# Pinning the order of TensorE's products in the attention of a two-mixer encoder layer

## The chip, the cores and the metric

One core of one Trainium2 chip runs one launch of the kernel. The metric is device microseconds of that launch: 922.22 us before the change, the median of 3 runs (920.89 to 922.51). Lower is better.

## The reference

One layer of a streaming encoder is applied to 512 prompt frames and 32 sample frames, 544 columns in all, with a model width of 1024. All data is float32.

```
h = rmsnorm(x)
z = h @ w_in            -> q_a k_a v_a q_b k_b v_b gate_a gate_b
q, k: RMS norm per head (head_dim 64)
mixer A: 16 q heads, 4 kv heads, own chunk of 64 and 2 before, ALiBi, a sink logit in the softmax
mixer B: 16 heads, own chunk and 8 before, learned bias by relative distance
x = x + (sigmoid(gate_a) * o_a + sigmoid(gate_b) * o_b) @ w_out
u = rmsnorm(x) @ w_up;  c = causal depthwise conv of width 3 over u;  [a | b] = c
x = x + (gelu(a) * b) @ w_down
```

It returns x and the new rows of the caches: k, v of both mixers and the last rows of u.

## The kernel before

Activations lie transposed, features on the 128 partitions and the 544 frames as columns. A projection (`dense`) makes 128 output features for all frames, in two halves of 272 columns. Every float32 operand is split into a rounded high part and a low rest, so each of the 8 blocks of a half takes three products (`triple`): high by high, high by low, low by high. A half is thus 24 products into one PSUM bank. The weights of a projection come by one DMA (`w_raw`), GpSimd rounds them (`w_hi`, L202; ScalarE does from the FFN on, L204), and VectorE makes the rest (`w_lo`, L205). Two buffers of each are there, so that a projection's weights are made while another's are used.

The first three projections run on rows that aren't normalised yet (`dense_first`), and are scaled when the norm is known. Somewhat later the rows are normalised in place (L255) and split again into the operands that the projections read (`row_split`, ScalarE L327, VectorE L328).

Attention is woven into the projections by hand. `Stream` has a clock of its own, which each queued product advances by its columns / 2350 us (at least 0.108; a transposition 0.109). A step of attention is a generator. It queues its products, then yields the time in which its next operands will be there (`LAT_...`), and is taken up again when the clock has come that far: `pe.step()` is called after each triple. The steps are these.

- `head_norm`: after each half of a q or k projection, ScalarE squares it (`t_sq`, L414), GpSimd splits the squares (`t_sqh`, `t_sql`, L416 and L417), and after `LAT_SQ` a product with `bdiag` sums them. ScalarE and VectorE make the root from it, GpSimd (L424) and VectorE (L425) scale, and q or k is written in two parts (L448, L449; L433, L434). `LAT_NORM` later it counts as ready, k after a further `LAT_DMA` for its copy to the other 64 partitions.
- `load_v`: `LAT_Z` after its projection v is transposed (L90).
- `attend_prompt`: a head's scores are made in four tiles, and VectorE adds the bias and finds the maxima (L504). The softmax (`nm` L485, exponentials L488, sums L492, reciprocal L494, scaling of p by GpSimd L496) is issued at a lower priority. `LAT_SOFT` later p is transposed (L90) and split (`pt_h`, `pt_l`, L514 and L515), and `LAT_PT` later come the products with v, an h part and an l part for each block, queued in one piece.
- `attend_sample` does the same for the 32 sample frames, with `LAT_SOFT_S` and `LAT_PTS`.

A head starts when its q, k and v are ready and `PACE_A` or `PACE_B` has passed since the one before. `reserve` holds a projection back while the buffers that it will need are taken. After the projections of mixer B (two for each group of gates at the end, `GATES_B`), `w_out` is begun while the last heads finish, and `pe.flush()` runs what is left.

The order so queued is not the order of the instructions on an engine. [...] 

The change touches the latencies (L55 to L59), `Stream`'s methods `matmul` and `transpose`, and the buffer counts in `head_norm`, `transposed` and `attend_prompt`.

Of the kernel before, what the change touches and what calls it, by code (L numbers as in the profile page):

```python
# [8 lines left out]
F32 = mybir.dt.float32  # L9
F32R = mybir.dt.float32r  # L10
# [42 lines left out]


LAT_FIRST, LAT_ROW = 9.15, 0.35  # L55
LAT_SQ, LAT_NORM, LAT_DMA = 2.9, 6.89, 3.63
LAT_Z, LAT_SOFT, LAT_PT = 6.55, 9.34, 4.75
LAT_SOFT_S, LAT_PTS = 8.46, 1.1
PACE_A, PACE_B, PACE_S = 7.09, 5.87, 1.44  # L59

WARM = 7
# [8 lines left out]
class Stream:  # L70
# [1 line left out]

    def __init__(self, nc):
        self.nc = nc
        self.clock, self.seq, self.next = 0.0, 0, 0.0
        self.tasks, self.heads = [], []
        self.live = {}

    def matmul(self, out, lhsT, rhs, **kw):
        n = 1
        for d in rhs.shape[1:]:
            n *= d
        self.clock += max(n / 2350, 0.108)
        return self.nc.tensor.matmul(out, lhsT=lhsT, rhs=rhs, **kw)  # L86

    def transpose(self, out, src, ident):
        self.clock += 0.109
        return self.nc.tensor.transpose(out, src, ident)  # L90

    def run(self, gen):
        for wait in gen:
# [50 lines left out]

def body(ctx, tc, a, o):
    nc = tc.nc
    pe = Stream(nc)
    mm, transpose = pe.matmul, pe.transpose
    act = nc.scalar.activation
    V, G = nc.vector, nc.gpsimd  # L150
# [11 lines left out]
    def bank(pool):  # L162
        return pool.tile([128, 512], F32, name="ps")
# [50 lines left out]
    def weights():  # L214
        n = state["used"]
        state["used"] += 1
        while state["prepped"] < min(n + 3, len(sources)):
            prep_next()
        return W.pop(n)

    def triple(ps, w, k, c0, cn, first, last):

        ks = slice(128 * k, 128 * k + 128)
        xs, xl = (x[:, c0:c0 + cn] for x in moving[k])
        mm(ps[:, :cn], lhsT=w[0][:, ks], rhs=xs, start=first, stop=False)
        mm(ps[:, :cn], lhsT=w[0][:, ks], rhs=xl, start=False, stop=False)
        mm(ps[:, :cn], lhsT=w[1][:, ks], rhs=xs, start=False, stop=last)
# [37 lines left out]
    def interleaved(halves, ks):  # L265

        for k in ks:
            for ps, w, s in halves:
                triple(ps, w, k, *HALVES[s], k == 0, k == KC - 1)
                pe.step()  # L270

    def dense_first(evac):


        early.append((evac, weights()))
        if len(early) < (FIRST if xt else 2):
            return
        halves = [(bank(psd if i < 3 else psa), early[i // 2][1], i % 2) for i in range(2 * len(early))]
        interleaved(halves[:3], range(KC))
        for h in halves[3:]:  # L280
            interleaved([h], range(KC))
        while not norm_done:
            pe.idle()
        for i, (ps, _, s) in enumerate(halves):
            c0, cn = HALVES[s]
            early[i // 2][0](s, c0, cn, ps[:, :cn])

    def leave(z, ps, c0, cn):

        if not scaled:  # L290
            state["left"] = V.tensor_tensor(z, ps, rstd[:, c0:c0 + cn], ALU.mult)
            return state["left"]
        return nc.scalar.copy(z, ps)
# [6 lines left out]
    ident = const.tile([128, 128], F32, name="ident")  # L300
# [12 lines left out]
    def newton(st, cn, pool):  # L313

        y = pool.tile([128, 272], F32, name="t_y")[:, :cn]
        act(y, st, AF.Ln, bias=eps)
        act(y, y, AF.Exp, scale=-0.5)  # L317
        b = pool.tile([128, 272], F32, name="t_b")[:, :cn]
        act(b, y, AF.Square)
        V.scalar_tensor_tensor(b, st, eps, b, ALU.add, ALU.mult)  # L320
        return b, y
# [9 lines left out]
    class RowNorm:  # L331


        def __init__(self, slots, tmp):
            self.slots, self.tmp, self.n, self.sums = slots, tmp, 0, []
            self.r = xp.tile([128, T], F32, name="rstd")
# [32 lines left out]
    ap = att.enter_context(tc.tile_pool(name="ap", bufs=2))  # L369
# [8 lines left out]
    xt = [slot() for _ in range(KC)]  # L378
# [24 lines left out]

    def head_norm(gi, write):
        def task(s, c0, cn, ps):
            z = ap.tile([128, 272], F32, name="z", bufs=4)[:, :cn]
            sq = ap.tile([128, 272], F32, name="t_sq", bufs=2)[:, :cn]
            sqh = ap.tile([128, 272], F32R, name="t_sqh")[:, :cn]
            sql = ap.tile([128, 272], F32R, name="t_sql")[:, :cn]
            gain = gains[:, gi:gi + 1]  # L410
            if not scaled:
                leave(z, ps, c0, cn)
                ps = z
            act(sq, ps, AF.Square)  # L414
            act(z, ps, AF.Identity, scale=gain)  # L415
            G.tensor_scalar(sqh, sq, 1.0, 1.0, ALU.mult, ALU.mult)  # L416
            G.tensor_tensor(sql, sq, rr(sqh), ALU.subtract)  # L417
            yield LAT_SQ
            st = bank(psa)[:, :cn]
            mm(st, lhsT=bdiag, rhs=sqh, start=True, stop=False)  # L420
            mm(st, lhsT=bdiag, rhs=sql, start=False, stop=True)
            b, y = newton(st, cn, ap)
            zn = ap.tile([128, 272], F32, name="zn")[:, :cn]
            G.tensor_tensor(z, z, y, ALU.mult)  # L424
            V.scalar_tensor_tensor(zn, b, -3.0, z, ALU.add, ALU.mult)  # L425
            write(s, c0, cn, zn)

        def evac(s, c0, cn, ps):
            pe.run(task(s, c0, cn, ps))
        return evac  # L430
# [67 lines left out]
    def scores(out, lhs, rhs, bias, floor, mx):  # L498
        ps = bank(psa)
        n = len(lhs)  # L500
        for i in range(n):
            mm(ps[:, :rhs[i].shape[1]], lhsT=lhs[i], rhs=rhs[i], start=i == 0, stop=i == n - 1)
        ps = ps[:, :out.shape[1]]
        V.tensor_tensor_reduce(out=out, in0=ps, in1=bias, op0=ALU.add, op1=ALU.max, scale=1.0,  # L504
                               scalar=floor, accum_out=mx)

    def transposed(p, blocks, n):

        ps = bank(psa)
        for src, dst in blocks:  # L510
            transpose(ps[:, dst:dst + 128], p[:, src:src + 128], ident)
        h = ap.tile([128, 512], F32R, name="pt_h", bufs=3)
        l = ap.tile([128, 512], F32R, name="pt_l", bufs=3)
        nc.scalar.copy(h[:, :n], ps[:, :n])  # L514
        V.tensor_tensor(l[:, :n], ps[:, :n], rr(h)[:, :n], ALU.subtract)  # L515
        return h, l

    def fold(po, dst, hh, n):

        own, other = ((slice(0, 64), slice(64, 128)), (slice(64, 128), slice(0, 64)))[hh]  # L520
        t = ap.tile([128, 512], F32, name="t_o", bufs=2)
        nc.scalar.copy(t[own, :n], po[other])
        V.tensor_tensor(dst[own], po[own], t[own, :n], ALU.add)
# [7 lines left out]
    def attend_prompt(q, kh, kl, bias, floor, sinkcol, geo, groups, vt, hh, dst, dh, scored, done):  # L531


        p = ap.tile([128, 1280], F32, name="p")
        mx = ap.tile([128, 4], F32, name="mx", bufs=4)
        tiles = []
        for t, (pc, k0, n, bc) in enumerate(geo):
            qs = q[:, 128 * t:128 * t + 128]
            scores(p[:, pc:pc + n], [qs, qs], [x[:, k0:k0 + max(n, 256)] for x in (kh, kl)], bias[:, bc:bc + n],
                   floor, mx[:, t:t + 1])  # L540
            tiles.append(slice(pc, pc + n))
        scored()
        with tc.high_priority(LATER):
            softmax(p, tiles, mx, sinkcol)
        yield LAT_SOFT
        pts = []
        for blocks, n, _ in groups:
            pts.append(transposed(p, blocks, n))
        yield LAT_PT
        po = bank(psa)  # L550
        started = False
        last = groups[-1][2][-1]
        for (h, l), (_, _, prods) in zip(pts, groups):
            for pr in prods:
                j, c, oc, w = pr
                for x in (h, l):
                    mm(po[:, oc:oc + w], lhsT=vt[:, j, hh, :, :], rhs=x[:, c:c + w],
                       start=not started, stop=pr is last and x is l, skip_group_check=True)
                    started = True
        fold(po, dst[:, :NP], dh, NP)  # L560
        done()
# [315 lines left out]
    for k in range(KC):  # L877
# [4 lines left out]
        if k >= lag:  # L882
            interleaved(halves[2:3], (k - lag,))
    pe.flush()
    interleaved(halves[2:3], range(KC - lag, KC))
    interleaved(halves[3:], range(KC))
    att.close()
# [18 lines left out]
    for i, (ps, _, s) in enumerate(halves):  # L906
        c0, cn = HALVES[s]
# [328 lines left out]
```

## Time and profile before

| | |
|---|---|
| median of 3 runs | 922.22 us (920.89 to 922.51) |
| the execution profiled | 921.02 us |
| its span, first to last instruction | 919.2 us |
| granted TensorE clock, mean | 0.996 |
| TensorE products busy | 895.1 us (97%), 7085 instructions |
| TensorE weight loads busy | 881.3 us (96%) |
| VectorE busy | 720.0 us (78%) |
| ScalarE busy | 540.5 us (59%) |
| GpSimd busy | 378.2 us (41%) |

PE stands for TensorE's products, PEld for its weight loads, DVE for VectorE, ACT for ScalarE, POOL for GpSimd. Products are pipelined and their ends are modelled, so they overlap in the records. Idle time of an engine counts in the waits only where it is over 0.15 us. Attention and its projections run to some 475 us; `w_out`'s remainder and the FFN follow.

### The profile page before, as it was taken

How to read it: one execution, taken by the hardware profiler on the slowest of the kernel's cores; microseconds unless marked ns; L12 is line 12 of the kernel's file. 1: busy time of each engine (PE TensorE's matmuls, PEld its weight loads, DVE VectorE, ACT ScalarE, POOL GpSimd, SP SyncE). 2: the span in 40 equal slices, each digit the busy share in tenths (PEclk: the TensorE clock that was granted, in tenths of full speed). 3: DMA queues.
4: the chain of work that ended last, by engine and by line, in shares of the span. 5: the costliest groups of instructions: out<-in, count | busy, mean ns of one | idle time of the engine just before them, and what ended most of it. 6: DMA issues, size and time to landing. Idle time of an engine off the chain costs nothing.

```text
span 919.2 us, 18903 instructions
## 1 busy us (share of the span) xinstructions
PE 895.1 (97%) x7085; PEld 881.3 (96%) x7085; DVE 720.0 (78%) x1470; ACT 540.5 (59%) x1283; POOL 378.2 (41%) x577
## 2 busy tenths in 40 slices
PE   7979999999999999999999999999999999999998
PEld 6979999989989999999999999999999999999998
DVE  7798867777988888997856568677787776886996
ACT  5668887778878677777663244334444433534542
POOL 4625548466867767765541213222222221100100
PEclk9999999999999999999999999999999999999999
DMA  7222133312344343343415222222222222232342
GB/s 223 90 89 87 53 96 92 112 58 82 109 133 125 113 145 106 124 126 120 134 47 189 83 79 92 93 92 80 82 93 92 92 90 76 93 107 78 117 146 67
DMA packets 40012, 94.38 MB, mean 103 GB/s; under 512 B 4944, under 2 KB 16240, under 8 KB 39920
## 3 DMA queue, kind: packets, MB, share of 16 engines
q1 hardware_dynamic: 39920, 93.17, 31.9%
q8 instruction: 56, 0.92, 0.4%
q14 instruction: 36, 0.29, 0.1%
HBM read 80.48 MB, written 7.10 MB: 95 GB/s over the span
## 4 chain that ended last, share of the span: by engine, by line
PE 78%; DVE 8%; ACT 3%; POOL 3%; issue 2%; DMA 0%; DVEq 0%; POOLq 0%; ACTq 0%
PE ps L86 75%; PE ps L90 3%; DVE q L449 1%; ACT p L488 1%; DVE w_lo L205 1%; DVE p L504 1%; POOL p L496 1%; DVE zn L425 1%; DVE s L255 1%; DVE t_b L320 1%; POOL t_sql L417 1%; DVE k L434 0%; POOL z L424 0%; DVE xl L328 0%; DMA k<-k 0%
## 5 line engine op out<-in xcount | busy, mean ns | idle before, releaser
L86 PE MATMUL ps<-xh,w_lo 128*128 128x272 f32 x1536 | 445.3, 291 | 5.6 <-DVE w_lo L205 5.6
L86 PE MATMUL ps<-xh,w_hi 128*128 128x272 f32 x1536 | 444.5, 291 | 2.8 <-ACT z L415 1.7
L86 PE MATMUL ps<-xl,w_hi 128*128 128x272 f32 x1536 | 444.5, 290 | 0.4 <-DVE xl L328 0.3
L86 PEld LDWEIGHTS ps<-xh,w_lo 128*128 128x128 f32 x1536 | 290.3, 189 | 7.0 <-DVE w_lo L205 6.5
L86 PEld LDWEIGHTS ps<-xh,w_hi 128*128 128x128 f32 x1536 | 290.1, 189 | 4.6 <-ACT z L415 1.9
L86 PEld LDWEIGHTS ps<-xl,w_hi 128*128 128x128 f32 x1536 | 290.6, 189 | 1.5 <-DVE xl L328 1.1
L205 DVE TENSOR_TENSOR w_lo<-w_raw,w_hi 128x1024 fp32r<-128x1024 f32 (+2 forms) x112 | 143.0, 1277 | 32.6 <-ACT w_hi L204 18.7
L202 POOL TENSOR_SCALAR w_hi<-w_raw 128x1024 fp32r<-128x1024 f32 (+2 forms) x62 | 67.0, 1082 | 92.9 <-PE ps L86 69.2
L496 POOL TENSOR_SCALAR p<-p,rc 128x256 f32<-128x256 f32 (+3 forms) x128 | 74.7, 601 | 41.3 <-DVE rc L494 37.9
L204 ACT CAST w_hi<-w_raw 128x1024 fp32r<-128x1024 f32 x50 | 52.6, 1051 | 64.8 <-issue 36.0
L86 PE MATMUL ps<-s,w_hi 128*128 128x272 f32 x448 | 84.0, 288 | 0.0
L488 ACT ACTIVATE p<-p,nm 128x256 f32<-128x256 f32 (+3 forms) x128 | 65.4, 513 | 28.0 <-DVE nm L485 27.9
L942 POOL TENSOR_SCALAR state_u<-u 128x2 f32<-128x2 f32 x44 | 17.1, 389 | 145.5 <-DVE u L939 145.5
L86 PE MATMUL ps<-s 128*128 128x272 f32 (+1 forms) x483 | 71.3, 293 | 1.7 <-DVE s L374 1.7
L86 PEld LDWEIGHTS ps<-s,w_hi 128*128 128x128 f32 x448 | 70.0, 188 | 0.0
L939 DVE TENSOR_TENSOR u<-ps,rstd 128x272 f32<-128x272 f32 x88 | 38.5, 440 | 39.6 <-PE ps L86 36.9
L86 PEld LDWEIGHTS ps<-s 128*128 128x128 f32 x483 | 65.0, 190 | 2.2 <-DVE s L374 1.7
L86 PE MATMUL ps<-s,w_lo 128*128 128x272 f32 x224 | 63.7, 288 | 0.0
L86 PE MATMUL ps<-k,q 128*128 128x256 f32 (+2 forms) x256 | 52.2, 308 | 3.3 <-DMA k<-k 1.6
L417 POOL TENSOR_TENSOR t_sql<-t_sq,t_sqh 128x272 fp32r<-128x272 f32 x52 | 52.6, 1012 | 3.7
L424 POOL TENSOR_TENSOR z<-z,t_y 128x272 f32<-128x272 f32 x52 | 42.7, 822 | 21.9 <-ACT t_y L317 19.9
L515 DVE TENSOR_TENSOR pt_l<-ps,pt_h 128x512 fp32r<-128x512 f32 (+1 forms) x80 | 45.6, 602 | 5.5 <-ACT pt_h L514 4.3
(164 smaller groups left out, 1627.3 us busy)
## 6 DMA issues: line engine op xcount, KB each, us to landing
w_raw<-in_w_in SPq DMA_DIRECT2D x50, 512.0 KB, 3.4
w_raw<-in_w_up SPq DMA_DIRECT2D x44, 512.0 KB, 3.3
w_raw<-in_w_pair SPq DMA_DIRECT2D x16, 512.0 KB, 3.3
k<-k SPq DMA_DIRECT2D x40, 128.0 KB, 2.3
bias<-in_rel SPq DMA_DIRECT2D x16, 256.0 KB, 2.9
w_raw<-in_w_out SPq DMA_DIRECT2D x8, 512.0 KB, 3.4
s<-in_x SPq DMA_DIRECT2D x15, 272.0 KB, 5.7
w_raw<-in_w_down SPq DMA_DIRECT2D x6, 512.0 KB, 3.3
```

Of the source, the lines that this page charges most:

```text
L86: return self.nc.tensor.matmul(out, lhsT=lhsT, rhs=rhs, **kw)
L90: return self.nc.tensor.transpose(out, src, ident)
L202: G.tensor_scalar(hi[:, c], raw[:, c], 1.0, 1.0, ALU.mult, ALU.mult)
L204: nc.scalar.copy(hi[:, c], raw[:, c])
L205: V.tensor_tensor(lo[:, c], raw[:, c], rr(hi)[:, c], ALU.subtract)
L417: G.tensor_tensor(sql, sq, rr(sqh), ALU.subtract)
L424: G.tensor_tensor(z, z, y, ALU.mult)
L488: act(p[:, sl], p[:, sl], AF.Exp, bias=nm[:, t:t + 1], accum_out=sm[:, t:t + 1])
L496: G.tensor_scalar(p[:, sl], p[:, sl], rc[:, t:t + 1], 1.0, ALU.mult, ALU.mult)
L515: V.tensor_tensor(l[:, :n], ps[:, :n], rr(h)[:, :n], ALU.subtract)
L939: V.tensor_tensor(u[:, 2 + c0:2 + c0 + cn], ps, rstd2[:, c0:c0 + cn], ALU.mult)
L942: G.tensor_scalar(state_u[:, m, 0:2], u[:, NP:NP + 2], 1.0, 1.0, ALU.mult, ALU.mult)
```

## The change

`Stream` takes the tile context and gets a flag, `strict`. While it is set, each product and each transposition that goes through `Stream` is passed to `keep_in_program_order`, which adds an edge of order, without a wait, to the engine's instruction traced before it. So TensorE's list is the order in which they were queued. The flag is set at the end of the first three projections, before their results are evacuated, and cleared after `pe.flush()`. The same function runs a second time for the FFN, where `xt` is empty and the flag stays off.

Seven of the latencies are raised, and seven tiles get more buffers.

```diff
-LAT_SQ, LAT_NORM, LAT_DMA = 2.9, 6.89, 3.63
-LAT_Z, LAT_SOFT, LAT_PT = 6.55, 9.34, 4.75
-LAT_SOFT_S, LAT_PTS = 8.46, 1.1
+LAT_SQ, LAT_NORM, LAT_DMA = 4.2, 8.0, 3.63
+LAT_Z, LAT_SOFT, LAT_PT = 7.0, 10.8, 5.4
+LAT_SOFT_S, LAT_PTS = 9.5, 2.3
...
-        return self.nc.tensor.matmul(out, lhsT=lhsT, rhs=rhs, **kw)
+        return self.keep(self.nc.tensor.matmul(out, lhsT=lhsT, rhs=rhs, **kw))
...
-        return self.nc.tensor.transpose(out, src, ident)
+        return self.keep(self.nc.tensor.transpose(out, src, ident))
+
+    def keep(self, product):
+        return self.tc.keep_in_program_order(product) if self.strict else product
...
         while not norm_done:
             pe.idle()
+        pe.strict = bool(xt)
...
-            z = ap.tile([128, 272], F32, name="z", bufs=4)[:, :cn]
-            sq = ap.tile([128, 272], F32, name="t_sq", bufs=2)[:, :cn]
-            sqh = ap.tile([128, 272], F32R, name="t_sqh")[:, :cn]
-            sql = ap.tile([128, 272], F32R, name="t_sql")[:, :cn]
+            z = ap.tile([128, 272], F32, name="z", bufs=6)[:, :cn]
+            sq = ap.tile([128, 272], F32, name="t_sq", bufs=3)[:, :cn]
+            sqh = ap.tile([128, 272], F32R, name="t_sqh", bufs=4)[:, :cn]
+            sql = ap.tile([128, 272], F32R, name="t_sql", bufs=4)[:, :cn]
...
-        h = ap.tile([128, 512], F32R, name="pt_h", bufs=3)
-        l = ap.tile([128, 512], F32R, name="pt_l", bufs=3)
+        h = ap.tile([128, 512], F32R, name="pt_h", bufs=4)
+        l = ap.tile([128, 512], F32R, name="pt_l", bufs=4)
...
-        p = ap.tile([128, 1280], F32, name="p")
+        p = ap.tile([128, 1280], F32, name="p", bufs=3)
...
     pe.flush()
+    pe.strict = False
```

Where no number of buffers is given, the pool's two are meant.

## Rows read from the trace of the kernel before

**Rows 1.** Windows: stretch and length, busy time (instructions) by engine, granted clock, DMA.
```profile
25.00:75.00 50.00, 43.76 (x330) 42.62 (x330) 44.70 (x92) 34.03 (x87) 19.50 (x25) 0.97 0.31 94
75.00:292.00 217.00, 210.12 (x1691) 205.74 (x1691) 173.32 (x423) 170.88 (x480) 140.25 (x191) 1.00 0.31 93
292.00:475.00 183.00, 180.02 (x1451) 174.97 (x1450) 154.35 (x337) 138.71 (x391) 122.54 (x151) 1.00 0.38 117
475.00:919.00 444.00, 440.88 (x3512) 440.32 (x3510) 329.05 (x586) 184.37 (x306) 83.65 (x197) 1.00 0.29 97
```

**Rows 2.** Chain of waits, its last long piece: start, length, what.
```profile
475.21 440.69 PE ps L86 x3510
```

**Rows 3.** Windows, sum of three: 260 to 292, 335 to 363, 420 to 475 us.
```profile
sum 115.00, PE 115.00 PEld 112.40 DVE 94.13 ACT 87.32 POOL 73.56; mean PE 38.33 PEld 37.47 DVE 31.38 ACT 29.11 POOL 24.52
```

**Rows 4.** TensorE's waits, largest of 25 to 75 and of 75 to 475 us.
```profile
PE ps L86 <- DVE w_lo L205: 4.3, 2, 3.0
...
PE ps L90 <- POOL p L496: 2.0, 3, 1.0
```

**Rows 5.** Timeline (start, length, engine, line), TensorE inside a head's second product.
```profile
219.62 0.29 PE L86 MATMUL ps<-xh,w_hi 128*128 128x272 f32 x1
...
220.75 0.28 PE L86 MATMUL ps<-pt_l,v 128*128 128x256 f32 x1
```

**Rows 6.** Timeline, a late step of squares: the projection's last product, the split squares.
```profile
390.95 0.28 PE L86 MATMUL ps<-xh,w_lo 128*128 128x272 f32 x1
...
393.67 0.95 POOL L417 TENSOR_TENSOR t_sql<-t_sq,t_sqh 128x272 fp32r<-128x272 f32 x1
```

**Rows 7.** Timeline, a late head: its last score, its last block of p.
```profile
380.76 0.63 PE L86 MATMUL ps<-k,q 128*128 128x512 f32 x2
...
391.58 0.70 POOL L496 TENSOR_SCALAR p<-p,rc 128x512 f32<-128x512 f32 x1
```

**Rows 8.** Timeline, squares near 87 us, by engine.
```profile
86.92 0.40 ACT L414 ACTIVATE t_sq<-ps 128x272 f32<-128x272 f32 x1
...
87.68 1.62 POOL L417 TENSOR_TENSOR t_sql<-t_sq,t_sqh 128x272 fp32r<-128x272 f32 x1
...
96.19 0.42 POOL L416 TENSOR_SCALAR t_sqh<-t_sq 128x272 fp32r<-128x272 f32 x1 [2.69 <-PE ps L86]
...
95.72 0.37 PE L86 MATMUL ps<-t_sqh,bdiag 128*128 128x272 f32 x1
```

**Rows 9.** Timeline, the first head: last score, sums, second splitting, p, first transposition.
```profile
55.42 0.50 PE L86 MATMUL ps<-k,q 128*128 128x256 f32 x2
...
71.03 0.16 DVE L492 TENSOR_TENSOR sm<-sm,es 128x4 f32<-128x4 f32 x1
...
72.72 1.74 DVE L328 SCALAR_TENSOR_TENSOR xl<-s,n,xh 128x272 fp32r<-128x272 f32 x4
...
76.76 3.86 POOL L496 TENSOR_SCALAR p<-p,rc 128x128 f32<-128x128 f32 x4 [1.38 <-DVE rc L494]
...
77.59 0.33 PE L90 MATMUL ps<-ident,p 128*128 128x128 f32 x1
...
80.04 0.44 PE L90 MATMUL ps<-ident,p 128*128 128x128 f32 x2 [0.99 <-POOL p L496]
```

**Rows 10.** Timeline after a wait for w_lo, and the window of one microsecond there.
```profile
66.44 0.60 PE L86 MATMUL ps<-xh,w_lo 128*128 128x272 f32 x1 [2.97 <-DVE w_lo L205]
...
69.79 0.33 PE L86 MATMUL ps<-xl,w_hi 128*128 128x272 f32 x1
...
67.00:68.00 1.00, 1.00 (x7) 1.00 (x6) 1.00 (x7) 1.00 (x5) 0.00 (x0) 0.50 0.62 131
```

**Rows 11.** Timeline, the last part of the first q, and a score.
```profile
53.10 1.30 DVE L449 TENSOR_TENSOR q<-zn,q 64x240 fp32r<-64x240 f32 x2
54.11 0.47 PE L86 MATMUL ps<-k,q 128*128 128x256 f32 x2 [0.47 <-DVE q L449]
```

**Rows 12.** GpSimd's waits from 75 to 475 us, the one for a buffer.
```profile
POOL t_sqh L416 <- PE ps L86: 2.7, 1, 2.7
```

More of the change, by code (lines that the diff above doesn't have):

```diff
@@ L70, with __init__ @@
 class Stream:
-    def __init__(self, nc):
-        self.nc = nc
+    def __init__(self, tc):
+        self.tc, self.nc = tc, tc.nc
+        self.strict = False
         self.clock, self.seq, self.next = 0.0, 0, 0.0
@@ L146, in body @@
     nc = tc.nc
-    pe = Stream(nc)
+    pe = Stream(tc)
     mm, transpose = pe.matmul, pe.transpose
```

## The prediction

> **What bounds the kernel now.** I read the busy times by stage first. In the FFN stretch (475 to 919 us) TensorE is busy 440.9 of 444 us, and the chain of waits runs through it for 440.69 us without another engine; the change ends before it. In the attention stretch TensorE is busy 210.1 of 217 and 180.0 of 183 us, and from 25 to 75 us 43.8 of 50 [rows 1, 2]. So the kernel is bound by TensorE, and what an order can win is its idle time: 9.9 us from 75 to 475 us and 6.2 us from 25 to 75. The weight loads see more, since a product that waits a little leaves a gap there: 174.97 + 205.74 = 380.7 busy of 400 us, 19.3 idle. Three quiet stretches of the same work, 115 us together, have 112.40 busy, 2.26% idle [rows 3]. At that rate 400 us would have 9.0 idle: the ceiling of a better order is 19.3 - 9.0 = 10.3 us.
>
> Then the waits, to see whose they are: from 25 to 75 us 4.3 of the 6.2 us are for w_lo, the weights' lower halves, while VectorE is busy 44.7 of 50 us; from 75 to 475 us they are many small ones, 2.0 us for normalised p the largest [rows 1, 4].
>
> Last the timeline, for the order itself. The second mixer product of a head (h and l parts of one list) is queued in one piece, yet nine projection products stand inside it from 219.62 to 220.75 us [rows 5]. So TensorE doesn't run the order in which Stream queues, but one that the compiler's scheduler made from its own estimate. That the pin changes nothing can be left aside.
>
> **The change part by part.** One profiled execution took 921.0 us (span 919.2); the sum is made against it, and the median shown is 922.2, so 1.2 is added at the end. A difference of 0.2%, 1.8 us, is about what can be told from none.
>
> *Part 1, the pin.* It adds and removes no product. From the end of the first three projections to flush(), a product that waits now holds all behind it: the projections, the evacuations that VectorE and ScalarE owe them, and the weights' buffers, which GpSimd and VectorE refill when TensorE is done. Before, ready projection products went ahead. So each attention product must be queued late enough. Stream's clock counts 272/2350 = 0.1157 us for a projection product; the rows give 440.69 us / 3510 = 0.1256 [rows 2]. One unit of its clock is thus about 1.085 us.
>
> *Part 2, the latencies.* Squares: 4.2, so 4.56 us. A late step: product starts at 390.95 and ends 0.28 later, its t_sql is written at 394.62, 3.4 us after: covered, by 1.2 us [rows 6]. Softmax: 10.8, so 11.7 us. A late head: last score ends at 381.39, last block of p at 392.28: 10.9 us, covered by 0.8 [rows 7]. The steps of mixer B resemble these, and I expect them to lose little.
>
> What the scheduler's order costs is seen at 87 us: t_sql is written at 89.30, but its product starts at 95.72, 6.4 us later, and only then has the next half's t_sqh (whose square was done at 87.32) its buffer, at 96.19, after 2.69 us of waiting for TensorE [rows 8]. In queued order the first product comes some 4.6 us after the projection and frees the buffer early. So a latency read from the profile of before is partly made by the displaced product, and the spikes should shrink.
>
> From 75 to 475 us I bound this term so. Below: the ceiling, -10.3 us. Above: two steps like the one at 87 us whose squares still come 10.5 us after the projection, 6 us too late each, 12 us, less the 6.9 us idle of 75 to 292 that such stands would replace [rows 1, 8]: +5. I take half of the ceiling, -5.1, as the covered late steps are most of the stretch and their covers are small.
>
> *Part 3, the start (25 to 75 us).* Here the latencies are far over what is queued. First softmax: scores end at 55.92, POOL multiplies p from 76.76 and the first transposition starts at 77.59, 21.7 us after [rows 9]. With its raised head start ((1.3 + 1.11) x 1.085 = 2.6 us later) TensorE reaches it at 55.92 + 2.6 + 11.7 = 70.2 us or later, and would stand to 77.6: 7.4 us. But the softmax is late by its low priority: its sums are added at 71.03, but GpSimd starts 5.7 us later, and in between VectorE splits normalised rows (72.72 us), in place of operands that the projections must have read first. Those projections now wait behind the transposition, so the splits can't go ahead of it. So the pin should bring it forward; at best TensorE doesn't stand. Between 0 and 7.4 I take 4.
>
> [...] So 4 + 1.6 = 5.6 us for the stand.
>
> The first head's scores ask for q, whose last part is written at 54.40, while the two tiles of the later half run at 54.11 and 55.42; TensorE ran projections between. Pinned, TensorE may stand for them: from nothing to 4 us, about half of the first softmax's stand; I take 1.5, near to the 1.3 us between the two tiles [rows 9, 11].
>
> Against this the w_lo wait of 2.97 us with its 1.6 us of lower clock goes or merges with the stand, as VectorE, nearly full in this stretch, catches up while TensorE stands: between 0 and -4.6, taken whole, as both fall within the same 10 us. The 1.0 us of waits for p at 80 us goes too. Sum of the start: 5.6 + 1.5 - 4.6 - 1.0 = +1.5.
>
> *Part 4, buffers.* z, squares, p and p transposed get 1 or 2 more buffers each. They cost no instruction. GpSimd waited for a buffer of t_sqh once, 2.7 us, from 75 to 475 [rows 12]; without the pin they would bring next to nothing. [...] The FFN's tiles take over attention's memory, now cut otherwise; they are hidden by the output projection, and if that cover goes it costs no more than one projection, 48 x 0.1256 = 6 us.
>
> *Part 5, the tail.* The last pair's chain (v, pace, softmax, p transposed) grows by (0.45 + 1.46 + 0.65) x 1.085 = 2.8 us. Four gate projections are queued behind it, 4 x 48 x 0.1256 = 24 us, and TensorE is busy all of 420 to 475 us now [rows 3]. Hidden: 0, at most +2.8.
>
> **Sum.** -5.1 + 1.5 + 0 + 0 = -3.6: 917.4 us for the execution profiled, 918.6 against the median.
>
> **Rivals.** *All of the ceiling.* The start costs nothing net and the rest of attention falls to the quiet rate: 922.2 - 10.3 = 911.9. For it: the 6.4 us that a ready product stood. Against it: VectorE, busy 327.7 of these 400 us, has its own bursts.
>
> *Slower: the pin stops TensorE at the first softmax.* The full 7.4 us and 1.6 us of lower clock, VectorE still behind afterwards, so that only 1 us of what I booked as recovered comes back, and 1.5 for scores: +9.5; then the rest of attention wins 2.5 instead of 5.1. Net +7.0: 929.2. It decides when p is still first multiplied near 76 us. For it: 21.7 us against 11.7. Against it: from 71.03 on the softmax waited in a queue, not for data.
>
> *No difference.* What attention wins, 5 us, the start gives back (a stand of about 7 us): 922.
>
> **How the numbers follow.** Forecast, -1.8 to -7: 0.33. Ceiling: 0.18. No difference: 0.20. Slower: 0.29. Faster is the first two, 0.51. The range goes from past the ceiling, with 4 us of waits at the start gone as well (922.2 - 14 = 908), to the slower rival with +2 of the tail (931). The forecast's own range is 915 to 920.4.
>
> **What would show it.** Right: the nine projection products inside a head's second product are gone; bdiag's product follows t_sql within about 2 us; TensorE's idle from 75 to 475 us falls from 9.9 to near 5 and its weight loads' from 19.3 to near 14; a stand of about 4 us before the first transposition, w_lo's of 2.97 us gone; the FFN at 444 us as before. Wrong: first p still at 76 us or later with TensorE standing, several stretches at half clock, or waits on t_sql and p after 75 us over 8 us together.

## The result, and the profile after

The change made the kernel slower: 943.02 us, the median of 4 runs (941.45 to 943.92), against 922.37 beside it. The ratio is 1.0228, 95% interval 1.021 to 1.0246. The forecast was 918.6 us and the range 908 to 931, so the time lies outside the range.

The execution profiled has a span of 940.5 us, 21.3 more than before, at a mean clock of 0.991. First the busy time by stage, the same columns as in [rows 1]:

```profile
25.00:75.00 50.00, 39.45 (x299) 38.55 (x298) 44.06 (x94) 31.34 (x80) 19.93 (x25) 0.95 0.32 98
75.00:292.00 217.00, 204.96 (x1605) 198.71 (x1606) 158.28 (x392) 165.13 (x460) 132.23 (x179) 0.98 0.27 85
292.00:515.00 223.00, 215.92 (x1715) 209.25 (x1713) 174.84 (x383) 159.30 (x434) 133.78 (x166) 1.00 0.37 118
515.00:940.00 425.00, 421.82 (x3361) 421.35 (x3360) 317.40 (x571) 174.61 (x292) 81.69 (x195) 1.00 0.28 93
```

TensorE's idle time up to 515 us is 10.55 + 12.04 + 7.08 = 29.7 us. Before it was 6.24 + 6.88 + 2.98 = 16.1 up to 475 us [rows 1]. The FFN is not touched. The last long piece of the chain of waits (start, length, what) answers to [rows 2]:

```profile
515.53 421.74 PE ps L87 x3360
```

421.74 / 3360 = 0.1255 us for a product, 0.1256 before. The piece before had 150 more products, so its equal began at 475.21 + 150 x 0.1256 = 494.0. Attention reaches that point 21.5 us later: the whole loss.

TensorE's waits from 25 to 515 us (total, times, longest) answer to [rows 4]:

```profile
PE ps L87 <- POOL t_sql L422: 7.4, 8, 1.1
PE ps L91 <- POOL p L501: 5.1, 2, 4.9
PE ps L87 <- DVE w_lo L209: 4.6, 2, 3.3
PE ps L87 <- DVE pt_l L520: 4.3, 4, 1.8
PE ps L91 <- DVE t_b L325: 1.8, 1, 1.8
PE ps L87 <- DVE s L528: 1.6, 3, 1.1
```

Lines of the same view of the kernel before, from 25 to 494 us:

```profile
PE ps L90 <- DVE t_b L320: 1.1, 1, 1.1
PE ps L86 <- POOL t_sql L417: 0.9, 2, 0.5
PE ps L86 <- DVE s L523: 0.8, 1, 0.8
```

The wait for w_lo stayed. New are eight stands of up to 1.1 us for the split squares, one of 4.95 us for the first p, and stands of scores and transpositions that end with a VectorE operation which reads a PSUM bank (`pt_l`, `s`, `mx`, `t_b`; none of these is an operand of the product that waits). I read them as waits for banks. From 76 us on, TensorE's stands of over 0.15 us come to 17.6 us: 7.7 for squares, 8.7 in 12 stands for such banks, 1.2 for the rest. Before, behind 80 us, they were 8.8: 1.6 for squares, 2.6 for such banks, 4.6 for the rest.

**The first softmax.** Timeline of the changed kernel, the first head; it answers to [rows 9]:

```profile
52.82 1.12 PE L87 MATMUL ps<-k,q 128*128 128x256 f32 x8
...
61.20 3.46 DVE L259 TENSOR_TENSOR s<-s,rstd 128x544 f32<-128x544 f32 x4
64.59 0.15 DVE L490 TENSOR_SCALAR nm<-mx 128x4 f32<-128x4 f32 x1
...
70.16 0.15 DVE L497 TENSOR_TENSOR sm<-sm,es 128x4 f32<-128x4 f32 x1
...
72.14 1.72 DVE L333 SCALAR_TENSOR_TENSOR xl<-s,n,xh 128x272 fp32r<-128x272 f32 x4
...
74.62 0.16 DVE L499 RECIPROCAL rc<-sm 128x4 f32<-128x4 f32 x1
...
75.80 0.48 PE L91 MATMUL ps<-ident,p 128*128 128x128 f32 x1 [4.95 <-POOL p L501]
```

The sums are ready at 70.3 us, but their reciprocal comes at 74.62. VectorE isn't idle in between: six splits of normalised rows (L333, 2.7 us in all, the largest group shown), a w_lo of 1.21 us and two evacuations stand ahead of it in its list. TensorE stands until the transposition at 75.80, and the first projection product behind the transpositions comes at 77.68.

**The lower clock.** After the stand for w_lo (3.28 us, to 65.92), from 66.1 to 69.5 us, and from 72.9 us, within this stand, to 79.8, the granted clock is 0.50. A third such stretch follows shorter stands, of 0.65 and 0.45 us. Windows, columns as in [rows 1], and two waits from TensorE's timeline:

```profile
75.80:79.60 3.80, 3.64 (x15) 3.02 (x16) 2.19 (x6) 2.44 (x8) 3.19 (x7) 0.50 0.00 0
...
107.00:110.50 3.50, 2.31 (x13) 1.70 (x13) 3.44 (x11) 2.98 (x8) 0.08 (x1) 1.00 0.16 67
...
110.50:113.90 3.40, 3.40 (x17) 3.34 (x16) 3.00 (x9) 1.42 (x5) 0.91 (x1) 0.50 0.07 13
...
107.70 1.09 PE L87 MATMUL ps<-k,q 128*128 128x256 f32 x4 [0.65 <-DVE t_b L325]
109.24 0.97 PE L87 MATMUL ps<-k,q 128*128 128x256 f32 x4 [0.45 <-DVE pt_l L520]
```

At 0.50 seven products start from 78.05 to 79.41 us, one every 0.227 us, against 0.125 at 1.00. So I count busy time there as half lost, an estimate from these two distances: 3.64 / 2 + 3.40 / 2 = 3.5 us for the two new stretches.

**The squares.** Timeline of the changed kernel near 455 us, GpSimd and then TensorE:

```profile
451.58 2.46 POOL L501 TENSOR_SCALAR p<-p,rc 128x128 f32<-128x128 f32 x4 [1.93 <-DVE rc L499]
454.02 0.41 POOL L421 TENSOR_SCALAR t_sqh<-t_sq 128x272 fp32r<-128x272 f32 x1
454.40 0.76 POOL L429 TENSOR_TENSOR z<-z,t_y 128x272 f32<-128x272 f32 x1
455.13 0.75 POOL L422 TENSOR_TENSOR t_sql<-t_sq,t_sqh 128x272 fp32r<-128x272 f32 x1
...
454.67 0.28 PE L87 MATMUL ps<-t_sqh,bdiag 128*128 128x272 f32 x1
455.94 0.39 PE L87 MATMUL ps<-t_sql,bdiag 128*128 128x272 f32 x1 [0.98 <-POOL t_sql L422]
```

GpSimd waits 1.93 us for a reciprocal, scales p, and puts another operation between t_sqh and t_sql. TensorE takes the first half's product and stands 0.98 us for the second.

Two more measures are worked out from the records of all products. *Excess*: each product's time to the next start, less the median for its kind before, summed. Over the whole span it rises from 38.5 to 59.8 us, which is the loss. From 25 to 80 us, where the half clock behind the first stand ends, it rises by 5.1, and by 16.3 behind that. Cut at 125 us it is 12.8 to 22.7 (+9.9), and in the rest 25.7 to 37.1 (+11.4). The changed kernel has done less of the work by either time, so such a split is rough. By the product before the gap, +10.7 stand behind scores and +7.6 behind the squares' first product. *Deferral*: from the end of t_sql to the start of its product. Its mean over 52 steps falls from 3.89 to 1.60 us. So the pin did bring the squares' products forward, and it didn't pay.

### The profile page after: what moved, and what is told of

Read it like the earlier page. It is cut to its first block, busy times and chain, and to the rows that moved or that the text cites. A ratio compares the mean times of both kernels' runs of the same rounds, so it can differ in the third digit from the quotient of the medians.

```text
span 940.5 us, 18834 instructions
## 1 busy us (share of the span) xinstructions
PE 902.3 (96%) x7085; PEld 885.3 (94%) x7085; DVE 713.0 (76%) x1470; ACT 542.9 (58%) x1283; POOL 379.4 (40%) x577
## 4 chain that ended last, share of the span: by engine, by line
PE 52%; ACT 2%; POOL 2%; DVE 1%; DMA 1%; issue 0%; SPq 0%; POOLq 0%; DVEq 0%
PE ps L87 51%; PE ps L91 1%; ACT p L493 1%; POOL p L501 1%; DMA s<-in_x 1%; DVE w_lo L209 0%; ACT s L624 0%; ACT L628 0%; ACT L624 0%; POOL w_hi L206 0%; POOL s L835 0%; POOL t_sql L422 0%; DVE nm L490 0%; DVE p L509 0%; DVE q L454 0%
## 5 line engine op out<-in xcount | busy, mean ns | idle before, releaser
L87 PE MATMUL ps<-xh,w_hi 128*128 128x272 f32 x1536 | 449.3, 294 | 1.3 <-ACT xh L332 1.3
L501 POOL TENSOR_SCALAR p<-p,rc 128x256 f32<-128x256 f32 (+3 forms) x128 | 72.3, 581 | 40.2 <-DVE rc L499 27.1
L945 DVE TENSOR_TENSOR u<-ps,rstd 128x272 f32<-128x272 f32 x88 | 38.5, 440 | 39.6 <-PE ps L87 37.0
L87 PE MATMUL ps<-k,q 128*128 128x256 f32 (+2 forms) x256 | 46.1, 311 | 8.7 <-DVE pt_l L520 4.3
L421 POOL TENSOR_SCALAR t_sqh<-t_sq 128x272 fp32r<-128x272 f32 x52 | 31.4, 604 | 46.9 <-ACT t_sq L419 46.6
```

What stands on the lines that cost most here:

```text
L87: return self.keep(self.nc.tensor.matmul(out, lhsT=lhsT, rhs=rhs, **kw))
L501: G.tensor_scalar(p[:, sl], p[:, sl], rc[:, t:t + 1], 1.0, ALU.mult, ALU.mult)
L945: V.tensor_tensor(u[:, 2 + c0:2 + c0 + cn], ps, rstd2[:, c0:c0 + cn], ALU.mult)
```

## The experiments

Each ratio is to the kernel before on the same chip. "Free" means without the pin, in the scheduler's order. The diffs are shortened ("..." marks what is left out) and are against the changed kernel, where nothing else is said.

### The three parts of the change

Buffers alone (latencies of before, no pin):

```diff
-LAT_SQ, LAT_NORM, LAT_DMA = 4.2, 8.0, 3.63
+LAT_SQ, LAT_NORM, LAT_DMA = 2.9, 6.89, 3.63
... (the other latencies as before, too)
-        pe.strict = bool(xt)
```

> Only the added buffers, latencies and free order as before. Theory (the loss of 20.7 us is the pinned order, at the start and in stands between products that follow each other): 922, within 3 us of before, as only one wait of GpSimd for a buffer (2.7 us) stood in the trace of before. Rival (the larger attention tiles move the FFN's tiles or free the scheduler for a worse order): 930 or more.

934.05 us, 1.0126 [1.0108, 1.0144]. A part that adds no instruction and that I priced at 0 costs 11.6 us.

Latencies and buffers, no pin:

```diff
-        pe.strict = bool(xt)
```

> Buffers and raised latencies, order not pinned. Theory: 919 to 926, the latencies alone only move attention some 3 us later behind projections that TensorE has anyway. Rival (the raised latencies make the heads late, and the tail and the reserved buffers pay): 932 or more.

940.94 us, 1.0201 [1.0179, 1.0224]. A loss of nearly the same size is there without the pin, but in another place: 12.3 of its 17.8 us of excess lie behind 300 us, while of the changed kernel's 21.4 us 14.8 lie before.

Pin and buffers, latencies of before:

```diff
-LAT_SQ, LAT_NORM, LAT_DMA = 4.2, 8.0, 3.63
+LAT_SQ, LAT_NORM, LAT_DMA = 2.9, 6.89, 3.63
... (the other latencies as before, too)
```

> Pinned order and buffers with the old, shorter latencies. Theory: worse than the change, 947 to 960, as each product comes 1 to 1.5 us earlier and stands that much longer. Rival (the raised latencies are the loss): 925 to 938, under the change's 943.

999.73 us, 1.0836 [1.0815, 1.0858], beyond the theory's 960. With short latencies TensorE stands 35 times for squares; its waits from 25 to 515 us:

```profile
PE ps L87 <- POOL t_sql L422: 21.1, 24, 2.9
PE ps L87 <- POOL t_sqh L421: 19.9, 11, 3.5
PE ps L91 <- POOL p L501: 12.2, 5, 6.5
```

So the longer latencies are needed with the pin. The next two have the buffers of before. Latencies alone, against the kernel before:

```diff
-LAT_SQ, LAT_NORM, LAT_DMA = 2.9, 6.89, 3.63
+LAT_SQ, LAT_NORM, LAT_DMA = 4.2, 8.0, 3.63
... (the other latencies as in the changed kernel, too)
```

> Only the raised latencies; order free, buffers as before. Theory (the added buffers let the scheduler put attention off behind projections, the latencies matter little): 920 to 926. Rival (raised latencies put the heads off by themselves): 928 to 934.

932.72 us, 1.0123 [1.0103, 1.0143]. Pin and latencies:

```diff
-            z = ap.tile([128, 272], F32, name="z", bufs=6)[:, :cn]
+            z = ap.tile([128, 272], F32, name="z", bufs=4)[:, :cn]
... (t_sq, t_sqh, t_sql, p, pt_h and pt_l as before, too)
```

> Pin and raised latencies with the buffers of before. Theory (buffers hurt only a free order; under the pin TensorE's list is the same with or without them): 940 to 948, like the change's 943. Rival (the buffers are the loss with the pin too): 928 to 934.

943.18 us, 1.0239 [1.0217, 1.0262]. With the pin and the new latencies the buffers do nothing, and TensorE runs the same list with either; without the pin they cost 11.6 us (alone) or 8 (beside the latencies). The pin costs 10.5 us beside the new latencies with the old buffers, 2 with the new ones, and 66 with the old latencies and the new buffers. Alone it was not run.

| | old buffers | new buffers |
|---|---|---|
| free, old latencies | 922 | 934.05 |
| free, new latencies | 932.72 | 940.94 |
| pinned, old latencies | not run | 999.73 |
| pinned, new latencies | 943.18 | 943.02 |

### Which buffers, and is the order before a lucky draw?

The squares' buffers alone, against the kernel before:

```diff
-            z = ap.tile([128, 272], F32, name="z", bufs=4)[:, :cn]
+            z = ap.tile([128, 272], F32, name="z", bufs=6)[:, :cn]
... (t_sq, t_sqh and t_sql as in the changed kernel, too)
```

> Order free, old latencies, more buffers for z and the squares alone. Theory (their buffers held a projection's evacuation back, and with it the projections, until the product of an earlier half had run): most of the 11.6 us of all added buffers, 929 to 935, and the product of the squares comes later after its operand than in before. Rival (p and its transposed parts are it): 920 to 925.

934.75 us, 1.0146 [1.0126, 1.0166].

Those of p and its transposed parts alone, against the kernel before:

```diff
-        p = ap.tile([128, 1280], F32, name="p")
+        p = ap.tile([128, 1280], F32, name="p", bufs=3)
... (pt_h and pt_l as in the changed kernel, too)
```

> Order free, old latencies, more buffers for p and its transposed parts alone. Theory (the buffers of the squares are the loss): 920 to 925. Rival: 929 to 935.

928.87 us, 1.0089 [1.0065, 1.0114]. Either set costs time alone, the squares' more; they don't add up. Small changes of the queue of the kernel before, with nothing else, test whether any new draw costs as much:

```diff
-LAT_Z, LAT_SOFT, LAT_PT = 6.55, 9.34, 4.75
+LAT_Z, LAT_SOFT, LAT_PT = 6.55, 9.34, 4.85
```

> Nothing of the change: the kernel before with LAT_PT 4.85 in place of 4.75, a shift of one transposed block by 0.1 of Stream's clock. Theory (the free order of before is one of many that small shifts give, and a favourable one; each of latencies and buffers alone gave 8 to 13 us more because it drew another): 926 to 935. Rival (each part of the change has a cost of its own, and a shift of 0.1 has none): 919 to 923.

923.48 us, 1.0021 [1.0005, 1.0037].

```diff
-PACE_A, PACE_B, PACE_S = 7.09, 5.87, 1.44
+PACE_A, PACE_B, PACE_S = 7.09, 5.97, 1.44
```

> The kernel before with PACE_B 5.97 in place of 5.87. Theory (another draw): 926 to 935, and not the same as the other shift's. Rival: 919 to 923.

923.01 us, 1.0016 [0.9998, 1.0033]. TensorE's list differs from before's from 310 and 275 us on, in 617 and 862 of 7085 places, yet the time hardly does. With the buffers alone it differs from 37 us on, in 2434 places, but 10.9 of their 13.8 us of excess lie behind 300 us too. So not every new draw in that stretch costs 11 us; two small ones don't rule out that the order before is a favourable one.

What the buffers and latencies also raise in the free order is the deferral. Its mean is 3.89 us before, and 3.76 and 3.88 with the two small changes, but 6.52 with the buffers alone, 7.22 with the squares' alone, 5.81 with p's alone and 6.07 with the latencies alone. It is no measure of the loss: latencies and buffers together have 5.47 and lose the most. Timeline with the buffers alone, GpSimd's t_sql and its product:

```profile
346.01 0.79 POOL L421 TENSOR_TENSOR t_sql<-t_sq,t_sqh 128x272 fp32r<-128x272 f32 x1
...
359.98 0.29 PE L87 MATMUL ps<-t_sql,bdiag 128*128 128x272 f32 x1
```

13.2 us pass between operand and product. A buffer that isn't free holds the next step's work back, as it did once for t_sqh before, 2.7 us [rows 12]. My reading is that it thereby also makes the scheduler finish the last step, and that more buffers let it prefer projections for longer. The deferrals fit that, but no run shows the scheduler's reason, nor that the deferral is what costs the time. The heads do lag: when the last gate projection ends, no attention product is left before, 5 are left with the buffers alone, and 21 with the latencies alone.

### Where the pinned order loses

Pin only from the point where both halves of the normalised rows are split:

```diff
-        pe.strict = bool(xt)
                 if n > RESCALE:
                     xt.clear()
+                    pe.strict = True
```

> The whole change, but the pin is set only when the second half of the normalised rows has been split (some 85 us), so the start runs as before. Theory A (the first softmaxes and the half clock after them are the loss): 930 to 933, 10 to 13 us under the change. Theory B (short stands all through attention are the loss): 937 to 941.

946.32 us, 1.0261 [1.0246, 1.0276], above both forecasts. A stand of 5.6 us for the first p, to 82.92 us, is still there. Pinning later doesn't take the loss away, but it doesn't take the start's stand away either, so the run doesn't tell what that stand is worth.

Score tiles of a head spread over the projections:

```diff
             tiles.append(slice(pc, pc + n))
+            if t < len(geo) - 1:
+                yield 0
```

> The whole change; a head's four score tiles are queued one triple of projection products apart, not in one piece. Theory (in the pinned order the scores stand for PSUM banks that VectorE and ScalarE have not read yet; time after score products grew by 9.6 us over before): 933 to 938. Rival (the banks come free no earlier, the stand only moves): 941 to 946.

948.32 us, 1.0296 [1.0272, 1.032]. The waits for p fall from 5.1 to 2.3 us, those for t_sqh and t_sql rise from 7.7 to 14.7.

Squares later:

```diff
-LAT_SQ, LAT_NORM, LAT_DMA = 4.2, 8.0, 3.63
+LAT_SQ, LAT_NORM, LAT_DMA = 5.6, 8.0, 3.63
```

> The whole change with LAT_SQ 5.6 in place of 4.2. Theory (the second product of the squares stands about 1 us for its operand in each of many steps; time after the first grew by 7.6 us over before): 935 to 939. Rival (a later product delays q and k, and the heads pay): 941 to 948.

946.85 us, 1.0274 [1.0252, 1.0296]. The waits for t_sql halve (7.4 to 3.5 us), but those for p (5.1 to 6.0), `mx` (1.3 to 2.9) and `s` (1.6 to 2.0) grow.

Transpositions queued one by one, with a triple of a projection between:

```diff
-        for src, dst in blocks:
+        for i, (src, dst) in enumerate(blocks):
+            if i or not first:
+                yield 0
             transpose(ps[:, dst:dst + 128], p[:, src:src + 128], ident)
... (those of v and of the samples' p likewise)
```

> The whole change; the transpositions of p, of p_s and of v are queued one by one, a triple of projection products between two. In the traces a transposition is followed after 0.109 us by another one, but after 0.028 us by a projection product; the pinned order has 292 adjacent pairs, the free order of before 221, this kernel 50. Theory (rows of transpositions are a part of the pinned order's loss): (292 - 50) x 0.081 = 19.6 us under the change, 923; with stands that move 925 to 932. Rival (as with the scores and the squares, time only moves, and each head's chain grows by some 4 us): 940 to 950.

968.32 us, 1.0506 [1.048, 1.0531]. The same with a single product between:

```diff
         mm(ps[:, :cn], lhsT=w[0][:, ks], rhs=xs, start=first, stop=False)
+        if norm_done:
+            pe.step()
... (and once more behind the triple's second product)
```

> As the kernel with transpositions one by one, and a step of attention may follow each product of a projection, not each triple: 10 adjacent pairs are left, and a head's transpositions take a third of the time. Theory: (292 - 10) x 0.081 = 22.8 us under the change, 920; with stands 918 to 928. Rival: 940 to 950.

963.49 us, 1.0466 [1.044, 1.0492]. Both are above even the rival's 950. The idea was wrong, as the timeline of the first of the two shows:

```profile
360.03 0.27 PE L91 MATMUL ps<-ident,p 128*128 128x128 f32 x1
360.06 0.37 PE L87 MATMUL ps<-xh,w_hi 128*128 128x272 f32 x1
360.26 0.29 PE L87 MATMUL ps<-xl,w_hi 128*128 128x272 f32 x1
360.39 0.29 PE L87 MATMUL ps<-xh,w_lo 128*128 128x272 f32 x1
360.51 0.27 PE L91 MATMUL ps<-ident,p 128*128 128x128 f32 x1
```

The next product starts 0.03 us after a transposition, but the one behind it 0.20 instead of 0.125. The cycle takes 0.48 us, three products (0.377) and 0.10 to 0.11 for the transposition. Nothing is saved by spreading. From 25 to 515 us the waits for squares grow from 7.7 to 16.8 us in the first and 16.2 in the second; that this comes of p's longer steps is my reading, and no run shows it.

### The other engines' lists

Four runs were meant to keep TensorE's list and to change only in which order VectorE, ScalarE and GpSimd take their work, three of them in the changed kernel and one in the kernel before. Only the softmax's edit did so. Squares at raised priority:

```diff
+            with tc.high_priority(SOONER):
                 G.tensor_scalar(sqh, sq, 1.0, 1.0, ALU.mult, ALU.mult)
                 G.tensor_tensor(sql, sq, rr(sqh), ALU.subtract)
```

> The changed kernel with GpSimd's two operations on the squares (t_sqh, t_sql) at raised priority in the lists that the scheduler makes; TensorE's list is the changed kernel's to the row. Theory (the pinned order is late because other work, as the scaling of p waiting for rc, stands between t_sqh and t_sql in GpSimd's list): the waits for t_sql fall from 7.4 us to under 3 and the time from 943 to 938 or less. Rival (the squares are late because GpSimd and ScalarE have no room, whatever the order of their lists): t_sql keeps 6 us or more, or what it loses appears on p; time 941 to 946.

943.61 us, 1.024 [1.0225, 1.0256], with the same waits. But near 455 us GpSimd's z still stands between t_sqh and t_sql, and in the trace all four engines take their instructions in the changed kernel's order from first to last:

```profile
453.90 0.42 POOL L422 TENSOR_SCALAR t_sqh<-t_sq 128x272 fp32r<-128x272 f32 x1
454.29 0.76 POOL L430 TENSOR_TENSOR z<-z,t_y 128x272 f32<-128x272 f32 x1
455.01 0.76 POOL L423 TENSOR_TENSOR t_sql<-t_sq,t_sqh 128x272 fp32r<-128x272 f32 x1
```

The edit moved nothing, so this run is the changed kernel again and decides nothing.

The prompts' softmax at normal priority:

```diff
-        with tc.high_priority(LATER):
-            softmax(p, tiles, mx, sinkcol)
+        softmax(p, tiles, mx, sinkcol)
```

> The changed kernel with the prompts' softmax at normal instead of lowered priority in the other engines' lists; TensorE's list is unchanged. Theory (the first transposition's stand of 4.95 us comes from the softmax's place in these lists): that stand falls below 1.5 us, the stretch at half clock at 72.9 us goes, time 936 to 940. Rival (the splits of normalised rows that are pushed back are asked for just as soon): the stand moves to w_lo or t_sql, time 942 or more.

961.36 us, 1.0436 [1.0421, 1.0452]. TensorE's waits from 25 to 515 us:

```profile
PE ps L87 <- POOL t_sql L422: 12.5, 10, 2.9
PE ps L87 <- POOL t_sqh L421: 8.5, 4, 3.1
PE ps L91 <- POOL p L501: 5.3, 2, 5.2
```

The first reciprocal still comes at 74.69 us, so the first stand stays, and those for squares grow from 7.7 to 21.0. With one and the same order on TensorE, the other engines' lists are worth 18 us. That the first stand comes of the splits ahead of the reciprocal isn't tested by it: VectorE's rows there are as they were. Both edits together:

> Both edits of the two lists at once on the changed kernel. If the orders of the other engines' lists make the stands of the pinned order: 930 to 936, near the kernel before. If these engines have no room: 941 or more.

961.06 us, 1.0434 [1.0416, 1.0451]; all four engines' lists are those of the softmax's edit alone. And the squares' edit on the kernel before:

> The kernel before, with GpSimd's two operations on the squares at raised priority; TensorE's list stays the kernel before's to the row. There a squares' product stands about 3.9 us behind its operands, so earlier operands bring nothing: 921 to 924. If the place of t_sql in GpSimd's list costs the free order too: 919 or less.

922.1 us, 1.001 [0.9999, 1.0021]. Here too all four lists are as before, so this run tests nothing.

## Why the prediction was wrong

The forecast of -3.6 was off by 24.9 us against the 21.3 that the profiled spans differ. By the excess, cut at 80 us, 3.6 of it lie in the start and 21.4 behind it; cut at 125 us, 8.4 and 16.5.

**Part 2 is the step that failed first**: "covered, by 1.2 us", from one step of squares at 391 us [rows 6]. From the records of all 52 steps, projection's last product to t_sql: before, the median is about 4.8 us and the upper quartile 6.8; the latency is 4.56. After, they are 3.7 and 5.5. I hoped the spikes would shrink, and they did, but 19 of the 52 steps are still later than queued. The trace of before had the spread; I took one row for it. The stands for squares rose from 1.6 to 7.7 us. The softmax's row was fairer: its median is 9.8 us, three quarters are under 11.2 before and 11.7 after, against a latency of 11.7.

**A term that the sum left out**: PSUM banks. In queued order a score or a transposition that finds its bank unread holds the projections behind it, and I priced nothing for that. These stands, read as above, rose from 2.6 to 8.7 us, a little more than those for squares.

**The stretch from 75 us on**: forecast -5.1, bounds -10.3 and +5. By the excess it is +16.3 behind 80 us and +11.4 behind 125, beyond the upper bound either way. That bound counted two late squares; from 76 us on there are 8 stands for t_sql, one for t_sqh and 14 of other kinds, 17.6 us in all, and a stretch at half clock at 110.5 us, estimated at 1.7 us, that I hadn't seen. Much of the idle time that they were to replace did go (ScalarE's z 1.7 us, the copy of k 1.6), but that is far less than what came. The rest of the excess lies in gaps too short to count as waits.

**Part 3, the start**: forecast +1.5, measured about +5.1 (to 80 us). The stand for p was sized well (4, measured 4.95), as was the half clock behind it (1.6, by the count above about 1.8). The 1.6 is what fourteen products of the kernel before lost at 0.50: 66.44 to 69.79 us is 3.35 us, against 14 x 0.1256 = 1.76 [rows 2, 10]. Wrong were two things. I booked back the w_lo wait with its clock, -4.6, whole; it is still there (3.28 us). And I wrote that the splits "can't go ahead of" the first transposition: six of them do go ahead of the reciprocal that it stands for, since VectorE's list is made by the scheduler and isn't pinned. The 1.5 for scores came to nothing, and the 1.0 of waits for p at 80 us went as forecast. My slower rival had the mechanism and the sign (first p at 75 us, TensorE standing), with +9.5 for the start; it missed the rest of attention, to which it gave -2.5, and ended 14 us under the time measured.

**Part 4, the buffers**: forecast 0, measured +11.6 us alone, and nothing beside the pin and the new latencies. So the 0 held in the sum by luck: the pin was there, and that was not my reason. I counted waits for buffers and not what their number does to the order that the scheduler makes. Nothing here shows too few of them before: GpSimd had one wait for a buffer, 2.7 us [rows 12], and more buffers brought no gain, pinned (943.02 us against 943.18) or free (934.05 against 922).

**Part 1, the pin**, did what it says: the squares' products follow sooner (1.60 us behind their operands with the pin, 5.47 without). That the free order comes of the scheduler's own estimate is my inference from [rows 5]; no run shows how it chooses. Beside the new latencies and buffers it moves the ratio from 1.0201 to 1.0228, and the intervals overlap: one loss took the place of another, behind 300 us without the pin and before it with the pin. Beside the new latencies and the old buffers it costs 10.5 us.

**Part 5**: TensorE is no longer full at the end of attention; the excess from 480 to 520 us is 2.4 us, and before, from 460 to 500, 0.5. The bound of +2.8 held, the 0 didn't.

**The FFN** was right (0.1255 us for a product).

What stays open is what the pinned order would be worth with lists to match on the other engines. That the lists matter is shown (18 us); that a better one exists is not, for the only edit that changed them made them worse. More PSUM banks for scores were not tried. No version tried is faster than the kernel before.

## What to carry to other kernels

Pinning TensorE's order moved the burden to the latencies (with the buffers 999.73 us with the old ones, 943.02 with the new) and to the order of the other engines (18 us between two sets of lists): read the spread of all steps of a kind, compare its upper quartile with the time allowed, and look where the producer stands in its own engine's list. Here a buffer count was also a rule of order (with the buffers alone 2434 of 7085 places of TensorE's list differ, and 11.6 us are lost): time buffers by themselves, even where they add no instruction. Before you read a run of another priority, compare the engines' lists: two of the edits here had changed none. Run a change of several parts part by part: here the buffers and the latencies each cost 11 us alone, which the time of the whole doesn't show.

## What the runs showed of the hardware

A transposition of 128 columns cost 0.10 to 0.11 us of TensorE here, in a row or alone (alone, what a cycle of 0.48 us has beside the 0.377 of its three products, as shown above). In the changed kernel ten in a row take 1.09 us in the chain of waits:

```profile
400.91 1.09 PE ps L91 x10
```

A lone one is followed after 0.03 us, but the product after next pays (0.20 for 0.125 us), as shown above. These ten are 0.109 us apart from start to start; their weight loads are recorded at 0.14 us each, overlapping, and no run shows what sets the distance.

The granted clock also fell to 0.50 where no long stand came before: from 107.0 to 110.5 us, still at 1.00, TensorE was busy 2.31 of 3.50 us, with stands of 0.65 and 0.45 us, and from 110.5 to 113.9 it ran at 0.50.
